# Reading 512-column products and scores from two places 1024 bytes apart, in a two-layer hybrid attention trunk on one Trainium2 core

## The chip, the cores and the metric

The kernel runs on one core of one Trainium2 chip. The time is the device time of one execution in microseconds, as the median of repeated runs. The profile is of one further execution. Its engines are called as in the trace: PE is TensorE's matrix multiply, PEld its weight load, DVE is VectorE, ACT is ScalarE, POOL is GpSimd and SP is SyncE, which issues the loads.

## The reference, cut to what matters

The program computes two layers over 256 tokens of width 1024 and a final RMS norm. Each layer normalises its input and multiplies it by one wide matrix. Out of that product come the queries, keys, values and gates of three causal attention mixers with 8 heads of 64 each, an index query and key, a weight per index head, a forget logit, and three merge gates.

```python
def hybrid_layer(x, gain, w_in, f_bias, w_branch, w_out):
    h = rms_norm(x, gain)
    proj = jnp.einsum('bsd,de->bse', h, w_in)
    # ... split into q, k, v, gate of a, b, c; q_idx, k_idx, w_idx; f_logit; merge_logit
    oa = moba_attention(...) * jax.nn.silu(ga)
    ob = dsa_attention(..., qi, ki, wi) * jax.nn.silu(gb)
    oc = forgetting_attention(...) * jax.nn.silu(gc)
    y = jnp.einsum('nbsw,nwd->bsnd', jnp.stack([oa, ob, oc], axis=0), w_branch)
    gates = jax.nn.sigmoid(merge_logit).reshape(B, S, N_BRANCH, D_MODEL)
    merged = jnp.sum(gates * y, axis=2)
    return x + jnp.einsum('bsd,de->bse', merged, w_out)
```

At 256 tokens mixer a is plain causal attention, mixer b keeps the 64 keys per query with the highest index score, which is a weighted sum over 8 index heads of relu(q_idx . k_idx), and mixer c adds a forgetting bias.

## The kernel before, in words

Everything is held to near float32 precision with products in a faster float format. A float32 operand is split into a high part, which ScalarE writes, and a low part, which VectorE gets by subtraction (`piece`, L345 to L368, for weights; `split_to`, L390, for activations). Each product is then three: high by high, low by high, high by low. So each weight piece of 128 x 1024 costs one instruction at L362 and one at L366, and three matmuls for each block of 128 rows.

Two functions make nearly all products. `unit_b` (L419) has the weights as the stationary operand and streams the 256 token columns of the normalised input; it makes queries, keys, gates and merge gates. `unit_a` (L435) has 128 tokens as the stationary operand and streams 512 weight columns; it makes the values of the mixers (`v_units`, L908) and the output projection (`w_out`), where the last 512 columns of the last token block are made as two units of 256. Both go through `mm_ops` (L401), so their matmuls all carry line L407. The values of the very first mixer are made by `first_v` (L922, matmuls at L954), which interleaves both token blocks as the weights arrive. `unit_y` (L833) makes the branch products.

The order in which a matmul reads its moving operand is a matter of the view. `turns` (in `hybrid_trunk`) turns a row of columns into pairs: column 0 of the first half, column 0 of the second half, column 1 of the first half, and so on. In `unit_b` and `unit_y` all 256-column products read this way already, from two places 512 bytes apart; their result lies pairwise in PSUM, and the readers undo it with `tiles`, which reads every second column (`plain` is the matching view of the destination). Products of 512 columns read their columns in order.

`scores` (L564) makes the scores of two heads against keys in one matmul: the key tile `bd` holds the two heads' keys 1024 bytes apart in each partition. For the first 128 queries it streams 2 x 128 columns, for the last 128 queries 2 x 256, three products each (L573 to L575). The result has head 0 in the first half and head 1 in the second. `attend` (L626) reads a head's scores with a VectorE instruction that adds the mask and takes the row extreme (L636), ScalarE takes the exponential (L640), the probabilities are transposed on TensorE (L663), split and multiplied by the values (L678 to L681). `index_scores` (L769) uses the same scores for the index heads: ScalarE writes the relu to an SBUF tile (L776, L777), VectorE sums the heads (L785, L787), and `select` (L790) takes the 64 highest by eight rounds of two instructions (L807, L808).

`v_out` (L915) writes the values' high and low parts to the tile `V` (L919, L920). The residual is added at L1039.

The order of the work is fixed ahead by a planner (`Plan.run`, L138). Each operation has a key, an engine and a price, and the planner simulates the engines and at each step writes out, on the engine that can start first, the ready operation of lowest key. A matmul's price is `t_mm` (L230), in ns for n columns. Buffers are taken and released in the same simulation, so a price moves the order on every engine.

At the end stands `forms` (L1047): 24 products of old data that nobody reads, in several read orders, planned behind everything else. The three buffers that they write are in turn s, s and t for every four products: 256 columns from four places and from eight places in turn, 256 columns from two places 1024 bytes apart, then 512 columns from two places 1024 bytes apart, from four places, and from two places 512 bytes apart within each half.

Of the kernel before, what the change touches and what calls it, by code (L numbers as in the profile page):

```python
# [227 lines left out]


def t_mm(n):  # L230
    return 1.3 + 0.4434 * n


@with_exitstack
def hybrid_trunk(ctx, tc, x, norm_gain, w_in, forget_bias, w_branch, w_out, final_gain, consts, out):
# [199 lines left out]
    def unit_a(name, gets, t, ah, al, ra, c=0, n=512):  # L435
        u = unit(name)
        ps = Buf("proj")
        o = lambda: T(ps)[:, :n]
        for i in range(4):
            p = gets[i](u)  # L440
            g = []
            for k in (2 * i, 2 * i + 1):
                wh = lambda p=p, k=k: p[0].v[:, k % 2, c:c + n]
                g += [(lambda k=k: ah(k, t), wh, [p[0]] + ra[0](k)), (lambda k=k: al(k, t), wh, [p[0]] + ra[1](k))]
            for k in (2 * i, 2 * i + 1):
                wl = lambda p=p, k=k: p[1].v[:, k % 2, c:c + n]
                g += [(lambda k=k: ah(k, t), wl, [p[1]] + ra[0](k))]
            mm_ops(o, g, t_mm(n), [ps], u, name, i == 0, i == 3, True)
        return u, ps
# [114 lines left out]
    def scores(q, k, ktoks, key):  # L564
        s0, s1 = Buf("s"), Buf("s")
        kt = [t for h in ktoks for t in h]

        def go():
            qh, ql = T(q[0]), T(q[1])
            kh, kl = T(k)  # L570
            for o, sl, n in ((T(s0)[:, :256], slice(0, 128), 128), (T(s1), slice(128, 256), 256)):
                o = o.rearrange("p (h c) -> p h c", h=2)
                PE.matmul(o, qh[:, sl], kh[:, :, :n], start=True, stop=False)  # L573
                PE.matmul(o, ql[:, sl], kh[:, :, :n], start=False, stop=False)  # L574
                PE.matmul(o, qh[:, sl], kl[:, :, :n], start=False, stop=True)  # L575
        pe(go, 3 * (t_mm(256) + t_mm(512)), [q[0], q[1], k] + kt, [s0, s1], key, "qk", MARGIN)
        return s0, s1

    class Pair:
# [46 lines left out]
        def attend(self, key):  # L626
            bs = [self.bias(h, key) for h in range(2)]
            s0, s1 = scores(self.q, self.k, self.kt, key)
            es, ke = [], []
            for h in range(2):  # L630
                b, bt, bb = bs[h]
                e, st = Buf("e"), Buf("st")
                kt = [Tok(), Tok()]
                parts = ((0, 0, 128, s0), (1, 128, 256, s1))
                for t, a, n, s in parts:
                    dve(lambda t=t, a=a, n=n, s=s, e=e, st=st, b=b, h=h: DVE.tensor_tensor_reduce(  # L636
                        T(e)[:, a:a + n], T(s)[:, h * n:(h + 1) * n], b()[:, a:a + n], 1.0, 3e38, ALU.add, ALU.min,
                        T(st)[:, t:t + 1]), n, [s, bt[t]], [kt[t]], key, "max", touch=[e, st] + bb)
                for t, a, n, s in parts:
                    act(lambda t=t, a=a, n=n, e=e, st=st: ACT.activation(  # L640
                        T(e)[:, a:a + n], T(e)[:, a:a + n], AF.Exp, bias=T(st)[:, t:t + 1], scale=-1.0,
                        accum_out=T(st)[:, 2 + t:3 + t]), n, False, [], [kt[t]], key, "exp", 185.0, touch=[e, st])
                for t, a, n, s in parts:
                    dve(lambda t=t, st=st: DVE.reciprocal(T(st)[:, 4 + t:5 + t], T(st)[:, 2 + t:3 + t]), 1, [], [kt[t]],
                        key, "recip", 75.0, touch=[st])

                    def on_act(t=t, a=a, n=n, e=e, st=st):
                        ACT.activation(T(e)[:, a:a + n], T(e)[:, a:a + n], AF.Copy, scale=T(st)[:, 4 + t:5 + t])

                    def on_dve(t=t, a=a, n=n, e=e, st=st):  # L650
                        DVE.tensor_scalar(T(e)[:, a:a + n], T(e)[:, a:a + n], T(st)[:, 4 + t:5 + t], None, op0=ALU.mult)  # L651
                    plan.op([("DVE", 129.0 + 0.52 * n, on_dve), ("ACT", t_act(n, False) + 93.0, on_act)], [], [kt[t]],
                            key, 0.0, "normalise", touch=[e, st]).port = True
                es.append(e)
                ke.append(kt)
            ph, pl = Buf("pth"), Buf("ptl")
            kp = [[Tok(), Tok()] for _ in range(2)]
            for h in range(2):
                ps = Buf("t")

                def tr(h=h, ps=ps):
                    for i in range(3):
                        PE.transpose(T(ps)[:, i * 128:(i + 1) * 128], T(es[h])[:, i * 128:(i + 1) * 128], ident)  # L663
                pe(tr, 330.0, ke[h] + [k_id], [ps], key, "pT", MARGIN, touch=[es[h]])
                src = lambda ps=ps: T(ps)[:, :384]
                act(lambda h=h, src=src: ACT.activation(T(ph)[:, h], src(), AF.Copy), 384, True, [ps],  # L666
                    [kp[h][0]], key, "pT", touch=[ph])
                dve(lambda h=h, src=src: DVE.tensor_tensor(T(pl)[:, h], src(), T(ph)[:, h].bitcast(F32), op=ALU.subtract),  # L668
                    384, [ps, kp[h][0]], [kp[h][1]], key, "pT", touch=[ph, pl])
            o = Buf("o")  # L670
            v = V[self.vi]

            def av():
                for h in range(2):
                    hd = 2 * self.p + h
                    ov = T(o)[:, h * S:(h + 1) * S]
                    a, b = slice(0, 256), slice(256, 384)
                    PE.matmul(ov, v[:, 0, hd], T(ph)[:, h, a], start=True, stop=False, skip_group_check=True)  # L678
                    PE.matmul(ov[:, 128:], v[:, 1, hd], T(ph)[:, h, b], start=False, stop=True, skip_group_check=True)
                    PE.matmul(ov[:64, 128:], v[:, 1, hd, :64], T(pl)[:, h, b], start=False, stop=False, skip_group_check=True)  # L680
                    PE.matmul(ov[:64], v[:, 0, hd, :64], T(pl)[:, h, a], start=False, stop=True, skip_group_check=True)  # L681
            kv = [t for p in k_V[self.vi] for t in p]
            pe(av, 700.0, kv + [ph, pl] + [t for h in kp for t in h], [o], key, "av", MARGIN)
            self.o, self.o_key = o, key
            if hasattr(self, "g"):
                self.gated()
# [82 lines left out]
    def index_scores(p, ps, kb, ktoks, key):  # L769
# [8 lines left out]
        for h in range(2):  # L778
            hd = 2 * p + h
            for t, (a, n) in enumerate(((0, 128), (128, 256))):  # L780
                rr = rel[t][:, h * n:(h + 1) * n]
                w = widx[:, t, hd:hd + 1]
                o = isc[:, a:a + n]
                if hd == 0:
# [128 lines left out]
            v_out(ps, t, vi, [ps], u)  # L913

    def v_out(ps, t, vi, deps, key):  # L915
        hi, lo = V[vi][:, t, :, :64], V[vi][:, t, :, 64:]
        src = lambda: T(ps).rearrange("p (h c) -> p h c", h=8)
        kv = [k for i in (2 * t, 2 * t + 1) for k in k_V[vi][i]]
        act(lambda: ACT.activation(hi, src(), AF.Copy), W, True, deps, kv, key, "v", touch=[ps])  # L919
        dve(lambda: DVE.tensor_tensor(lo, src(), hi.bitcast(F32), op=ALU.subtract), W, deps, kv, key, "v", touch=[ps])  # L920
# [1 line left out]
    def first_v():  # L922
# [5 lines left out]
        for i in range(4):  # L928
# [19 lines left out]
            for t in range(2):  # L948
                for w, h, kw, kx in ((ph, hA[0], kh, 0), (ph, hA[1], kh, 1), (pl, hA[0], kl, 0)):
                    for j in ((0,), (1,)) if i == 0 else ((0, 1),):  # L950
                        def emit(t=t, w=w, h=h, j=j, i=i, v3=v3):
                            for x in j:
                                left[t][0] -= 1
                                PE.matmul(T(ps[t]), h(2 * i + x, t), v3(w)[:, x], start=left[t][0] == 23, stop=left[t][0] == 0)  # L954
                        k = Tok()
                        done[t].append(k)
                        pe(emit, len(j) * t_mm(512), [kw[x] for x in j] + [k_hT[kx][t][2 * i + x] for x in j], [k], us[t] - 10,
# [41 lines left out]
    for l in range(L):  # L999
# [30 lines left out]
        for hh in range(2):  # L1030
            gets = [lambda k, i=i: rows_a("O", w_out, l, hh * 512, i, k) for i in range(4)]
            for t in range(2):
                ra = [lambda k, p=p: [k_mg[k][p]] for p in range(2)]
                cols = [(0, 256), (256, 256)] if last and hh + t == 2 else [(0, 512)]
                for i, (c, n) in enumerate(cols):
                    u, ps = unit_a(f"o{hh}{t}", gets, t, mA[0], mA[1], ra, c, n)
                    c += hh * 512
                    o = xs[t][:, c:c + n]
                    dve(lambda o=o, ps=ps, n=n: DVE.tensor_tensor(o, o, T(ps)[:, :n], op=ALU.add), n, [ps], [k_x[t][hh]],  # L1039
                        u - 4, "res")  # L1040
                    if last:
                        final_part(t, c, n, hh + i, u - 4, i == 1)
# [4 lines left out]
    def forms():  # L1047
# [4 lines left out]
        def emit():  # L1052
            bs = [T(x) for x in b]
            n = 0

            def go(m, w, v, k):
                nonlocal n
                for i in range(k):
                    x = v(f[:, i * w:(i + 1) * w])
                    y = x.shape  # L1060
                    o = bs[n % 3][:, :m]
                    o = o.rearrange("p (b a) -> p b a", a=y[2]) if len(y) == 3 else o.rearrange("p (c b a) -> p c b a", b=y[2], a=y[3])
                    PE.matmul(o, hTh[:, i, :128], x, start=True, stop=True)
                n += 1
            go(256, 256, lambda x: x.rearrange("p (a b) -> p b a", a=4), 4)
            go(256, 256, lambda x: x.rearrange("p (a b) -> p b a", a=8), 4)
            go(256, 512, lambda x: x.rearrange("p (a b) -> p b a", a=2)[:, :128], 4)
            go(512, 512, lambda x: x.rearrange("p (a b) -> p b a", a=2), 4)
            go(512, 512, lambda x: x.rearrange("p (a b) -> p b a", a=4), 4)
            go(512, 512, lambda x: x.rearrange("p (c a b) -> p c b a", c=2, a=2), 4)  # L1070
        pe(emit, 5000.0, [k_main] + hT_all[0] + hT_all[1], b, 10 ** 6, "forms")
    forms()
    PLAN_T.append(plan)
    PLAN_T[0] = plan.run({"PE": 0.0, "ACT": 0.0, "DVE": 0.0})
# [25 lines left out]
```

## Time and profile before

| | |
|---|---|
| median of 3 runs | 629.85 us (629.82 to 631.39) |
| profiled execution | 630.21 us |
| its span, first to last instruction | 628.4 us |
| TensorE busy | 615.5 us, 98% |
| VectorE busy | 543.7 us, 87% |
| ScalarE busy | 400.0 us, 64% |
| GpSimd busy | 85.4 us, 14% |
| granted TensorE clock | 1.0 |
| read from memory | 103.69 MB |

The span is what the views of the trace are measured in; the profiled execution's own time is 1.8 us longer, which lies outside the program's instructions. The chain of work that ended last is followed back from the last instruction, each time to what released it. Matmuls are pipelined: the length printed for one covers time in which the next already runs, so a product's price is read from the distance of starts.

### The profile page before, as it was taken

How to read it: one execution, taken by the hardware profiler on the slowest of the kernel's cores; microseconds unless marked ns; L12 is line 12 of the kernel's file. 1: busy time of each engine (PE TensorE's matmuls, PEld its weight loads, DVE VectorE, ACT ScalarE, POOL GpSimd, SP SyncE). 2: the span in 40 equal slices, each digit the busy share in tenths (PEclk: the TensorE clock that was granted, in tenths of full speed). 3: DMA queues.
4: the chain of work that ended last, by engine and by line, in shares of the span. 5: the costliest groups of instructions: out<-in, count | busy, mean ns of one | idle time of the engine just before them, and what ended most of it. 6: DMA issues, size and time to landing. Idle time of an engine off the chain costs nothing.

```text
span 628.4 us, 12640 instructions
## 1 busy us (share of the span) xinstructions
PE 615.5 (98%) x4860; PEld 584.3 (93%) x4860; DVE 543.7 (87%) x1334; ACT 400.0 (64%) x797; POOL 85.4 (14%) x98
## 2 busy tenths in 40 slices
PE   7999989999999999999999998999999999999999
PEld 6999989899998999899889998998999999999988
DVE  8899998986978989899588999989698898989873
ACT  5775576666756667575487656767567674847641
POOL 1342120100000221200004303020000012211001
PEclk9999999999999999999999999999999999999999
DMA  8845638455472562665545545565736455363701
GB/s 295 275 144 163 202 100 270 136 168 172 149 251 68 177 193 68 201 216 187 155 150 184 170 136 166 158 212 167 227 109 202 137 161 160 107 210 101 267 34 68
DMA packets 93853, 105.56 MB, mean 168 GB/s; under 512 B 4320, under 2 KB 82400, under 8 KB 93792
## 3 DMA queue, kind: packets, MB, share of 16 engines
q1 hardware_dynamic: 93504, 104.36, 52.1%
q8 instruction: 38, 0.62, 0.4%
q10 hardware_dynamic: 288, 0.39, 0.2%
q14 instruction: 23, 0.19, 0.1%
HBM read 103.69 MB, written 1.05 MB: 167 GB/s over the span
## 4 chain that ended last, share of the span: by engine, by line
PE 71%; DVE 21%; ACT 4%; DMA 2%; issue 1%; SPq 0%; ACTq 0%; DVEq 0%
PE proj L407 61%; DVE wl L366 8%; PE t L663 2%; ACT e L640 2%; DVE isc L808 2%; PE proj L954 2%; DVE t L807 1%; DMA raw<-in_w_out_dram 1%; PE s L573 1%; PE s L575 1%; PE s L574 1%; DVE rsh L455 1%; DVE rr L457 1%; DVE isc L787 1%; DVE e L636 1%
## 5 line engine op out<-in xcount | busy, mean ns | idle before, releaser
L366 DVE TENSOR_TENSOR wl<-raw,wh 128x1024 fp32r<-128x1024 f32 (+1 forms) x190 | 234.7, 1247 | 30.9 <-ACT wh L362 29.7
L407 PE MATMUL proj<-hTh,wh 128*128 128x256 f32 (+1 forms) x1040 | 247.0, 277 | 2.1 <-DVE g L602 1.7
L407 PE MATMUL proj<-hTl,wh 128*128 128x256 f32 (+1 forms) x1040 | 245.7, 275 | 0.0
L362 ACT ACTIVATE wh<-raw 128x1024 fp32r<-128x1024 f32 (+1 forms) x190 | 197.8, 1055 | 71.2 <-PE proj L407 49.1
L407 PEld LDWEIGHTS proj<-hTh,wh 128*128 128x128 f32 (+1 forms) x1040 | 199.0, 191 | 3.9 <-DVE g L602 2.5
L407 PEld LDWEIGHTS proj<-hTl,wh 128*128 128x128 f32 (+1 forms) x1040 | 199.2, 192 | 0.7
L407 PE MATMUL proj<-hTh,wl 128*128 128x256 f32 (+1 forms) x1040 | 160.1, 277 | 0.0
L407 PEld LDWEIGHTS proj<-hTh,wl 128*128 128x128 f32 (+1 forms) x1040 | 137.9, 191 | 1.3
L456 POOL TENSOR_TENSOR rsh<-rsh,cst 128x256 f32<-128x256 f32 (+1 forms) x42 | 35.3, 840 | 380.0 <-DVE rsh L455 380.0
L640 ACT ACTIVATE e<-e,st 128x128 f32<-128x128 f32 x96 | 42.6, 445 | 19.3 <-DVE st L636 19.2
L458 POOL TENSOR_TENSOR rr<-rr,rsh 128x256 f32<-128x256 f32 (+1 forms) x42 | 43.4, 1032 | 15.6 <-ACT mth L824 6.0
L407 PE MATMUL proj<-wh,v 128*128 128x512 f32 (+1 forms) x144 | 35.6, 368 | 0.0
L407 PE MATMUL proj<-og0l,wh 128*128 128x256 f32 x128 | 32.2, 277 | 0.3 <-DVE og0l L398 0.3
L407 PE MATMUL proj<-wh,hTh 128*128 128x512 f32 x80 | 32.3, 404 | 0.0
L407 PE MATMUL proj<-og0h,wh 128*128 128x256 f32 x128 | 32.1, 277 | 0.0
L407 PE MATMUL proj<-wh,hTl 128*128 128x512 f32 x80 | 31.5, 394 | 0.0
L694 ACT ACTIVATE ot<-o 64x256 f32<-64x256 f32 x48 | 18.3, 381 | 19.5 <-PE o L681 19.0
L407 PEld LDWEIGHTS proj<-wh,v 128*128 128x128 f32 x144 | 25.2, 188 | 4.7
L663 PE MATMUL t<-cst,e 128*128 128x128 f32 x144 | 24.5, 279 | 1.8 <-DVE e L651 1.2
L668 DVE TENSOR_TENSOR ptl<-t,pth 128x384 fp32r<-128x384 f32 x48 | 25.2, 550 | 0.7 <-ACT pth L666 0.3
L407 PEld LDWEIGHTS proj<-og0l,wh 128*128 128x128 f32 x128 | 24.6, 192 | 0.7 <-DVE og0l L398 0.5
L407 PE MATMUL proj<-wl,hTh 128*128 128x512 f32 x80 | 24.9, 392 | 0.0
(195 smaller groups left out, 1023.8 us busy)
## 6 DMA issues: line engine op xcount, KB each, us to landing
raw<-in_w_in_dram SPq DMA_DIRECT2D x74, 1024.0 KB, 5.2
raw<-in_w_branch_dram SPq DMA_DIRECT2D x24, 512.0 KB, 4.9
raw<-in_w_out_dram SPq DMA_DIRECT2D x8, 1024.0 KB, 5.8
raw<-in_w_in_dram SPq DMA_DIRECT2D x3, 512.0 KB, 7.1
x<-in_x_dram SPq DMA_DIRECT2D x4, 256.0 KB, 4.5
raw<-in_w_in_dram SPq DMA_DIRECT2D x2, 320.0 KB, 5.8
out_dram<-tmp SPq DMA_DIRECT2D x2, 320.0 KB, 2.4
raw<-in_w_in_dram SPq DMA_DIRECT2D x2, 256.0 KB, 4.4
```

Of the source, the lines that this page charges most:

```text
L362: ACT.activation(p[0].v, sel(c.v), AF.Copy)
L366: DVE.tensor_tensor(p[1].v, sel(c.v), p[0].v.bitcast(F32), op=ALU.subtract)
L407: PE.matmul(o(), a(), b(), start=first and i == 0, stop=last and i == n - 1)
L455: dve(lambda: DVE.stream_shuffle(T(sh)[:np_], a(), SWAP), S, [ps], [sh], key, "rope")
L456: gps(lambda: POOL.tensor_tensor(T(sh)[:np_], T(sh)[:np_], s[:np_], op=ALU.mult), S, [k_rope], [sh], key, "rope")
L458: gps(lambda: POOL.tensor_tensor(T(r)[:np_], T(r)[:np_], T(sh)[:np_], op=ALU.add), S, [sh], [r], key, "rope")
L640: act(lambda t=t, a=a, n=n, e=e, st=st: ACT.activation(T(e)[:, a:a + n], T(e)[:, a:a + n], AF.Exp, bias=T(st)[:, t:t + 1], scale=-1.0, acc ...
L663: PE.transpose(T(ps)[:, i * 128:(i + 1) * 128], T(es[h])[:, i * 128:(i + 1) * 128], ident)
L668: dve(lambda h=h, src=src: DVE.tensor_tensor(T(pl)[:, h], src(), T(ph)[:, h].bitcast(F32), op=ALU.subtract), 384, [ps, kp[h][0]], [kp[h][1 ...
L694: act(lambda r=r, h=h: ACT.activation(T(t)[r], T(o)[64:, h * S:(h + 1) * S], AF.Copy), S, True, [o], [kt[h]], key, "og", HALF, touch=[t])
L808: dve(lambda o=o, t8=t8: DVE.match_replace(o, T(t8), o, TAKEN), n, [t8], [k_isc[i]], key + r * step, "top8")
L954: PE.matmul(T(ps[t]), h(2 * i + x, t), v3(w)[:, x], start=left[t][0] == 23, stop=left[t][0] == 0)
```

## The change: what it does

Products of 512 columns in `unit_a` and `first_v` read their columns through `turns`, so from two places 256 columns, that is 1024 bytes, apart in turn. The two `unit_a` units of 256 columns at the end read from two places 512 bytes apart. The result lies pairwise in PSUM: `v_out` and the residual add read it with a step of two columns. In `scores` the keys of the two heads are read in turn, and the result has the heads in turn; the score maximum at L636 and the index sum at L785 and L787 read every second column.

The planner's price of a product changes: for 256 columns from 114.8 to 111.6 ns, for 512 from 228.3 to 216.3 ns. The unread products at the end are others: 28 in place of 24.

```diff
 def t_mm(n):
-    return 1.3 + 0.4434 * n
+    return 7.0 + 0.4087 * n
...
     def unit_a(name, gets, t, ah, al, ra, c=0, n=512):
-        o = lambda: T(ps)[:, :n]
+        o = lambda: T(ps)[:, :n].rearrange("p (b a) -> p b a", a=2)
...
-                wh = lambda p=p, k=k: p[0].v[:, k % 2, c:c + n]
+                wh = lambda p=p, k=k: turns(p[0].v[:, k % 2, c:c + n])
...
-                wl = lambda p=p, k=k: p[1].v[:, k % 2, c:c + n]
+                wl = lambda p=p, k=k: turns(p[1].v[:, k % 2, c:c + n])
...
     def scores(q, k, ktoks, key):
-                o = o.rearrange("p (h c) -> p h c", h=2)
-                PE.matmul(o, qh[:, sl], kh[:, :, :n], start=True, stop=False)
-                PE.matmul(o, ql[:, sl], kh[:, :, :n], start=False, stop=False)
-                PE.matmul(o, qh[:, sl], kl[:, :, :n], start=False, stop=True)
+                o = o.rearrange("p (c h) -> p c h", h=2)
+                mh, ml = (x[:, :, :n].rearrange("p h c -> p c h") for x in (kh, kl))
+                PE.matmul(o, qh[:, sl], mh, start=True, stop=False)
+                PE.matmul(o, ql[:, sl], mh, start=False, stop=False)
+                PE.matmul(o, qh[:, sl], ml, start=False, stop=True)
...
     def attend(self, key):
-                        T(e)[:, a:a + n], T(s)[:, h * n:(h + 1) * n], b()[:, a:a + n], 1.0, 3e38, ALU.add, ALU.min,
+                        T(e)[:, a:a + n], T(s)[:, :2 * n].rearrange("p (c h) -> p h c", h=2)[:, h], b()[:, a:a + n], 1.0, 3e38, ALU.add, ALU.min,
...
     def index_scores(p, ps, kb, ktoks, key):
-                rr = rel[t][:, h * n:(h + 1) * n]
+                rr = rel[t].rearrange("p (c h) -> p h c", h=2)[:, h]
...
     def v_out(ps, t, vi, deps, key):
-        hi, lo = V[vi][:, t, :, :64], V[vi][:, t, :, 64:]
-        src = lambda: T(ps).rearrange("p (h c) -> p h c", h=8)
+        hi, lo = (V[vi][:, t, :, c:c + 64].rearrange("p (a h) c -> p a h c", a=2) for c in (0, 64))
+        src = lambda: T(ps).rearrange("p (h c a) -> p a h c", h=4, a=2)
...
     def first_v():
-                                PE.matmul(T(ps[t]), h(2 * i + x, t), v3(w)[:, x], start=left[t][0] == 23, stop=left[t][0] == 0)
+                                PE.matmul(T(ps[t]).rearrange("p (b a) -> p b a", a=2), h(2 * i + x, t), turns(v3(w)[:, x]), start=left[t][0] == 23, stop=left[t][0] == 0)
...
-                    dve(lambda o=o, ps=ps, n=n: DVE.tensor_tensor(o, o, T(ps)[:, :n], op=ALU.add), n, [ps], [k_x[t][hh]],
+                    dve(lambda o=o, ps=ps, n=n: DVE.tensor_tensor(plain(o), plain(o), tiles(T(ps)[:, :n]), op=ALU.add), n, [ps], [k_x[t][hh]],
...
     def forms():
-            go(256, 256, lambda x: x.rearrange("p (a b) -> p b a", a=4), 4)
-            go(256, 256, lambda x: x.rearrange("p (a b) -> p b a", a=8), 4)
-            go(256, 512, lambda x: x.rearrange("p (a b) -> p b a", a=2)[:, :128], 4)
-            go(512, 512, lambda x: x.rearrange("p (a b) -> p b a", a=2), 4)
-            go(512, 512, lambda x: x.rearrange("p (a b) -> p b a", a=4), 4)
-            go(512, 512, lambda x: x.rearrange("p (c a b) -> p c b a", c=2, a=2), 4)
-        pe(emit, 5000.0, [k_main] + hT_all[0] + hT_all[1], b, 10 ** 6, "forms")
+            go(256, lambda i: f[:, i * 256:i * 256 + 256].rearrange("p (c a b) -> p c b a", c=2, a=2), 4)
+            go(256, lambda i: f[:, i * 64:i * 64 + 768].rearrange("p (a b) -> p b a", a=2)[:, :128], 4)
+            go(256, lambda i: f[:, i * 64:i * 64 + 1024].rearrange("p (a b) -> p b a", a=2)[:, :128], 4)
+            go(256, lambda i: f[:, i * 256:i * 256 + 264].rearrange("p (a b) -> p b a", a=2)[:, :128], 4)
+            go(256, lambda i: f[:, i * 256:i * 256 + 288].rearrange("p (a b) -> p b a", a=2)[:, :128], 4)
+            go(512, lambda i: f[:, i * 64:i * 64 + 1024].rearrange("p (a b) -> p b a", a=2)[:, :256], 4)
+            go(128, lambda i: f[:, i * 256:i * 256 + 128].rearrange("p (a b) -> p b a", a=2), 4)
+        pe(emit, 4000.0, [k_main] + hT_all[0] + hT_all[1], b, 10 ** 6, "forms")
```

More of the change, by code (lines that the diff above doesn't have):

```diff
@@ L1054, in emit, with go @@
             n = 0
-            def go(m, w, v, k):
+            def go(m, v, k):
                 nonlocal n
                 for i in range(k):
-                    x = v(f[:, i * w:(i + 1) * w])
+                    x = v(i)
                     y = x.shape
                     o = bs[n % 3][:, :m]
-                    o = o.rearrange("p (b a) -> p b a", a=y[2]) if len(y) == 3 else o.rearrange("p (c b a) -> p c b a", b=y[2], a=y[3])
+                    if len(y) == 3:
+                        o = o.rearrange("p (b a) -> p b a", a=y[2])
+                    elif len(y) == 4:
+                        o = o.rearrange("p (c b a) -> p c b a", b=y[2], a=y[3])
                     PE.matmul(o, hTh[:, i, :128], x, start=True, stop=True)
                 n += 1
-            go(256, 256, lambda x: x.rearrange("p (a b) -> p b a", a=4), 4)
-            go(256, 256, lambda x: x.rearrange("p (a b) -> p b a", a=8), 4)
-            go(256, 512, lambda x: x.rearrange("p (a b) -> p b a", a=2)[:, :128], 4)
-            go(512, 512, lambda x: x.rearrange("p (a b) -> p b a", a=2), 4)
-            go(512, 512, lambda x: x.rearrange("p (a b) -> p b a", a=4), 4)
-            go(512, 512, lambda x: x.rearrange("p (c a b) -> p c b a", c=2, a=2), 4)
-        pe(emit, 5000.0, [k_main] + hT_all[0] + hT_all[1], b, 10 ** 6, "forms")
+            go(256, lambda i: f[:, i * 256:i * 256 + 256].rearrange("p (c a b) -> p c b a", c=2, a=2), 4)
[6 more added lines that the diff above has]
+        pe(emit, 4000.0, [k_main] + hT_all[0] + hT_all[1], b, 10 ** 6, "forms")
     forms()
```

## The prediction

> **What bounds the kernel now.** I read the page's busy line and its chain of work first, then the busy time by stretches cut where the chain changes engine, then the matmuls in order of time.
>
> ```profile
> span 628.4 us, 12640 instructions
> PE 615.5 (98%) x4860; PEld 584.3 (93%) x4860; DVE 543.7 (87%) x1334; ACT 400.0 (64%) x797; POOL 85.4 (14%) x98
> PE 71%; DVE 21%; ACT 4%; DMA 2%; issue 1%; SPq 0%; ACTq 0%; DVEq 0%
> ```
>
> TensorE is busy nearly all the time and carries 71% of the chain; VectorE carries 21%. The next view, busy time in stretches, shows where (columns: stretch, length, then PE, PEld, DVE, ACT, POOL busy with instruction counts, granted clock, DMA share, GB/s):
>
> ```profile
> 47.70:87.50 39.80, 37.16 (x315) 36.01 (x315) 39.59 (x120) 22.17 (x41) 9.81 (x12) 1.00 0.53 165
> 87.50:223.70 136.20, 136.18 (x1109) 130.71 (x1108) 117.25 (x273) 89.80 (x186) 9.92 (x11) 1.00 0.55 174
> 223.70:253.20 29.50, 28.53 (x248) 27.66 (x246) 27.21 (x73) 21.06 (x46) 6.04 (x8) 1.00 0.35 103
> 284.60:359.90 75.30, 75.25 (x504) 68.20 (x505) 61.21 (x129) 48.69 (x83) 12.91 (x15) 1.00 0.51 161
> 359.90:391.80 31.90, 30.32 (x261) 29.49 (x260) 31.77 (x108) 17.03 (x31) 5.83 (x9) 1.00 0.52 163
> 391.80:530.70 138.90, 138.88 (x1134) 133.50 (x1133) 118.84 (x276) 90.73 (x188) 11.53 (x13) 1.00 0.54 171
> ```
>
> In the long stretches (136, 75 and 139 us) TensorE never rests and VectorE has 14 to 20 us to spare: a shorter matmul there ends the stretch sooner. In the selection stretches (40 and 32 us) VectorE is full (39.59 of 39.80) and TensorE waits some 2 us in each: a shorter matmul there only waits longer. The clock is 1.00 everywhere, so matmul time is set by the instruction, not by throttling.
>
> **What a product costs now, and in the new order.** A busy matmul's printed length overlaps the next one, so I use distances between starts. The tail of the timeline holds all the forms needed. First the last output products in order of time (columns: start, length, engine, line, names, shape, count), then a look at 625.0 us that separates two of the unread products at L1063:
>
> ```profile
> 606.74 1.08 PE L407 MATMUL proj<-wh,v 128*128 128x512 f32 x4
> ...
> 616.40 0.63 PE L407 MATMUL proj<-wh,v 128*128 128x256 f32 x4
> ...
> 622.06 1.61 PE L1063 MATMUL s<-hTl,hTh 128*128 128x256 f32 x8
> 623.49 0.63 PE L1063 MATMUL t<-hTl,hTh 128*128 128x256 f32 x4
> 623.96 2.15 PE L1063 MATMUL s<-hTl,hTh 128*128 128x512 f32 x8
> 625.94 1.03 PE L1063 MATMUL t<-hTl,hTh 128*128 128x512 f32 x4
> ```
>
> ```profile
> 624.83 0.43 PE L1063 MATMUL s<-hTl,hTh 128*128 128x512 f32 x1
> ```
>
> From 606.74 to 616.40 the program issues 42 products of 512 contiguous columns: 9.66 us / 42 = 230 ns each. From 616.40 to 622.06 there are 48 of 256 contiguous columns: 5.66 / 48 = 118 ns. The unread products at L1063 already contain the new order: the first four of 512 columns read two places 256 elements, that is 1024 bytes, apart in turn, and take 623.96 to 624.83, 217 ns each. The next four, which go through four places, take 624.83 to 625.94, 278 ns. So not every order is good, but the one chosen is 13 to 14 ns below the contiguous one. (The eight products of 256 columns at 622.06, four and eight places in turn, average 179 ns.) That the gain survives beside the other engines' traffic is seen from the 256-column products, which already alternate between places 512 bytes apart: one piece of the chain of waits (start, length, what),
>
> ```profile
> 174.85 9.39 PE proj L407 x84
> ```
>
> is 9.39 / 84 = 112 ns each in the middle of the kernel, against 118 contiguous.
>
> The counts, from the instruction groups by shape (count | busy us, mean ns | idle before):
>
> ```profile
> L407 PE MATMUL proj<-wh,hTh 128*128 128x512 f32 x80 | 32.3, 404 | 0.0
> L407 PE MATMUL proj<-wh,v 128*128 128x512 f32 x112 | 30.5, 394 | 0.0
> L407 PE MATMUL proj<-wh,v 128*128 128x256 f32 x32 | 5.1, 280 | 0.0
> L954 PE MATMUL proj<-wh,hTh 128*128 128x512 f32 x16 | 5.4, 407 | 2.3 <-DVE small L478 1.6 <-ACT hTh L515 0.7
> L574 PE MATMUL s<-bd0h,ql 128*128 128x512 f32 x12 | 4.7, 395 | 0.0
> ```
>
> Each product is made of three terms (high by high, low by high, high by low), so values through unit_a are 3 x 80 = 240 products; the output is 112 + 56 = 168 of 512 columns and 32 + 16 = 48 of 256; first_v has 3 x 16 = 48. Scores are made 32 times (24 head pairs, 8 index pairs; the L574 row holds those of one of three key buffers), each with three products of 256 and three of 512 columns: 96 of each. The order inside one group of scores:
>
> ```profile
> 117.49 0.28 PE L575 MATMUL s<-bd1l,qh 128*128 128x256 f32 x1
> 117.61 0.39 PE L573 MATMUL s<-bd1h,qh 128*128 128x512 f32 x1
> 117.83 0.40 PE L574 MATMUL s<-bd1h,ql 128*128 128x512 f32 x1
> ```
>
> 120 ns for 256, 220 for 512 with the two-digit rounding of this view: the contiguous prices above within 10 ns. Their two heads also lie 1024 bytes apart; the third unread form (623.49, 256 columns from places 1024 bytes apart) takes 0.47 / 4 = 117 with its first product and I take 112, the price of the alternated 256 above.
>
> **The change part by part.**
>
> Values and output in unit_a: 408 products x 13.5 ns = 5.5 us, nearly all in stretches where TensorE sets the end. The 48 of 256 columns at the very end: 48 x 6 = 0.3 us, on the path.
>
> first_v: 48 x 13.5 = 0.65 us; its first half waits for weights and activations (the idle 2.3 us in its row), so 0.4.
>
> Scores: 96 x 13.5 + 96 x 6 = 1.9 us. Index scores and many attention scores lie in stretches that VectorE sets; I take half, 0.9, between ends of 0.3 and 1.9.
>
> Readers of the reordered results: v_out, the residual add and the score maximum now read every second PSUM column, the index sum L787 every second SBUF element. What such a read costs, from groups that already do it (the first of each pair reads with a step, the second does not):
>
> ```profile
> L398 DVE SCALAR_TENSOR_TENSOR ql<-proj,qh 128x256 fp32r<-128x256 f32 x8 | 3.4, 421 | 0.0
> L850 DVE SCALAR_TENSOR_TENSOR acc<-acc,proj 128x256 f32<-128x256 f32 x16 | 6.6, 414 | 0.4
> L397 ACT ACTIVATE qh<-proj 128x256 fp32r<-128x256 f32 x8 | 3.0, 374 | 2.0 <-PE proj L407 1.9
> L821 ACT ACTIVATE acc<-proj 128x256 f32<-128x256 f32 x16 | 6.1, 379 | 11.2 <-PE proj L407 11.2
> L397 ACT ACTIVATE v<-acc 128x256 fp32r<-128x256 f32 x16 | 7.2, 474 | 10.1 <-DVE acc L857 10.1
> L397 ACT ACTIVATE og0h<-ot 128x256 fp32r<-128x256 f32 x16 | 6.7, 417 | 7.7 <-DVE ot L699 6.7 <-POOL ot L698 0.8
> ```
>
> and the index sum as it is now:
>
> ```profile
> L787 DVE SCALAR_TENSOR_TENSOR isc<-tmp,widx,isc 128x256 f32<-128x256 f32 x14 | 7.7, 551 | 0.0
> ```
>
> From PSUM the step costs nothing on either engine (421 to 414, 374 to 379 ns), so the first three groups are put at 0; at 7 ns each the 96 maxima would cost 0.7 us. From SBUF it costs ScalarE 57 ns per 256. Index sums: 32, between 0 and 57 ns each, 0 to 1.8 us, inside the stretches VectorE sets; I take 0.8. The Trainium skill (SBUF — State Buffer, Door 1) says SBUF delivers 16-byte lines and that two hits in a line suffice; a step of 8 bytes would then be free, and this term 0. The ScalarE pair disagrees with it.
>
> The planner's matmul price falls from 114.8 to 111.6 ns for 256 columns and from 228.3 to 216.3 for 512. It writes out every engine's order, so some orders will shift. No row prices this; the nearest are TensorE's longest single waits for VectorE (engine, waiting line, cause: total us, times, longest):
>
> ```profile
> PE s L575 <- DVE bd1l L712: 2.0, 1, 2.0
> PE s L575 <- DVE bd2l L712: 1.3, 1, 1.3
> ```
>
> One such wait gained or lost: -2 to +2 us; I take 0, as the new price is nearer to the measured distances and points neither way.
>
> The unread products at the end: 24 become 28 (20 of 256, 4 of 512, 4 of 128 columns). They run behind the last output product, beside the final norm and the output transfer:
>
> ```profile
> L560 ACTq DMA_DIRECT2D out_dram<-tmp x2: 350/362/375, 620.0 to 624.8; - x2
> DMA to landing us min/median/max: 2.0/2.4/2.6
> ```
>
> The transfer issued at 624.8 lands by 627.4, while the last unread product ends at 625.94 + 1.03 = 627.0. The cover is 627.4 - 622.06 = 5.3 us. The new set takes 20 x 112 + 4 x 217 + 4 x 112 = 3.6 us, or with 179, 278 and 179 ns 5.4 us: 0 to 0.1 us; I take 0. It does move the last busy instruction, so the page's chain may end on another engine.
>
> Sum: 5.5 + 0.3 + 0.4 + 0.9 - 0.8 = 6.3 us off. The profiled execution took 630.2 us (span 628.4 and 1.8 around it), so 623.9; the median of the runs is 0.4 below that execution, so 623.5.
>
> **The rivals.**
>
> (1) VectorE takes over more. With TensorE faster, its 87% becomes 88%, and the stretches where both are over 90% grow; or a shifted order adds a wait like the two above. For it: PE stands still only some 2 us in each selection stretch, so the engines are close there. Against: the long stretches have 14 to 20 us of VectorE slack. Scores then bring nothing, a wait of 2 us comes in: 6.3 - 0.9 - 2 = 3.4 off, 626.5; 2 to 5 off in all.
>
> (2) Nothing arrives, within 0.3%: the alternated order costs the same once the weights are being written next to it. The 256-column rows speak against it. 629.9.
>
> (3) Slower: the score maximum (L636, 96 instructions) reads PSUM with a step in an operation that no row shows with one. At half speed (135 ns per 128 columns, from the rows below) a head costs 405 ns more, 48 heads 19.4 us of VectorE; with two fifths of it where VectorE sets the end (my choice between none and all), 8 us: 631.5. It decides from 6.3 / (0.4 x 48) = 330 ns per head on.
>
> ```profile
> L636 DVE CUSTOM_DVE_ANT_0 e<-s,cst 128x256 f32<-128x256 f32 x16 | 6.7, 417 | 0.0
> L636 DVE CUSTOM_DVE_ANT_0 e<-s,cst 128x128 f32<-128x128 f32 x16 | 4.5, 282 | 0.0
> ```
>
> (4) Slower by much: reading from two places loses time in each product, as four places do. At 278 instead of 230 ns, 552 products cost 26 us more: 656. The same section of the Trainium skill speaks for this: each access that leaves its line pays a penalty, and here every access does. By that rule the change loses; the four products at 623.96 and the 112 ns products show it does not hold for two places.
>
> **How the numbers follow.** The forecast (5 to 8.5 us off) gets 0.64, rival 1 0.24, rival 2 0.06, rival 3 0.04, rival 4 0.02. A measurement of this kernel tells 0.3%, 1.9 us, from no change. Faster is the forecast and rival 1: 0.88; same 0.07, with a little of rival 3; slower 0.05. Time 623.5. Upper end: rival 1 with the index sums at their 1.8 us, 627.2. Lower end: all of first_v and the scores, index sums free (8.3 us off), and half a wait gained, 620.6.
>
> **What would show it.** Distances of 217 ns between starts of 512-column products at L407 and L954, and of 112 in the last 48, would confirm the main term; 230 means rival 2, 278 rival 4. L636 at 417 and 282 ns refutes rival 3. L787 (551 ns for 256 now) shows the index term. TensorE's list of waits and the selection stretches (39.8 and 31.9 us now) show whether VectorE took the gain: if products cost 217 and the time falls by less than 5 us, the planner's order or VectorE is where it went. The forecast fails if the products get their price but long new waits on L712 or L366 appear.

## The result and the profile after

The changed kernel takes 619.37 us (618.74 to 620.75, 4 runs) against 629.84 us before (629.40 to 631.39, 4 runs): a ratio of 0.9832, 95% interval 0.9807 to 0.9858, or 10.5 us less. The forecast was 623.5 with a range of 620.6 to 627.2: the sign was right, the gain 1.7 times the predicted one, and the time lies under the range.

The page of the kernel after (span, busy time, chain by engine):

```profile
span 618.6 us, 12635 instructions
PE 606.7 (98%) x4864; PEld 584.7 (95%) x4864; DVE 540.0 (87%) x1319; ACT 407.0 (66%) x814; POOL 82.2 (13%) x96
PE 70%; DVE 20%; ACT 1%; issue 1%; ACTq 0%; DVEq 0%
```

The shares look as before, but one thing the edits of the reads did not touch has moved: VectorE has 15 instructions fewer, ScalarE 17 more, GpSimd 2 fewer. With the new prices the planner put work on other engines: the normalisation of the probabilities has a form for VectorE and one for ScalarE, and those on ScalarE (L649, L648 before) rise from 23 to 40; two gate products moved from GpSimd to VectorE.

The products have the price that the prediction read from the unread ones. The last output products in order of time, kernel after (start, length, engine, line, names, shape, count):

```profile
600.40 1.03 PE L407 MATMUL proj<-wh,v 128*128 128x512 f32 x4
...
606.87 0.61 PE L407 MATMUL proj<-wh,v 128*128 128x256 f32 x4
...
612.23 0.50 PE L1067 MATMUL s<-hTl,hTh 128*128 128x256 f32 x3
```

30 products of 512 columns from 600.40 to 606.87 are 216 ns each (230 before), 48 of 256 from 606.87 to 612.23 are 112 (118 before). The readers, by shape (count | busy us, mean ns | idle before), kernel after:

```profile
L637 DVE CUSTOM_DVE_ANT_0 e<-s,cst 128x256 f32<-128x256 f32 x16 | 6.7, 420 | 0.0
L637 DVE CUSTOM_DVE_ANT_0 e<-s,cst 128x128 f32<-128x128 f32 x16 | 4.5, 284 | 0.0
L788 DVE SCALAR_TENSOR_TENSOR isc<-tmp,widx,isc 128x256 f32<-128x256 f32 x14 | 7.0, 497 | 0.0
L788 DVE SCALAR_TENSOR_TENSOR isc<-tmp,widx,isc 128x128 f32<-128x128 f32 x14 | 5.8, 415 | 0.0
```

The score maximum reads every second PSUM column at 420 and 284 ns (417 and 282 before). The index sum, put at up to 57 ns more, got shorter: 497 ns from 551. The experiments show that the new order did this, and that the step by itself made it longer.

TensorE's waits of before at the scores, 2.0 and 1.3 us for L712, are gone from its list; of what is left there, the longest and the one at the scores are these (engine, waiting line, cause: total us, times, longest):

```profile
PE proj L407 <- DVE wl L366: 2.3, 3, 1.4
PE proj L955 <- DVE wh L945: 1.7, 1, 1.7
...
PE s L576 <- DVE bd0l L713: 0.5, 1, 0.5
```

So the products explain part, and an order with fewer waits may explain the rest. The experiments take the two apart. Each run is compared with runs of the kernel before on the same chip, which lay between 630.0 and 630.4 us in the median. In some executions the granted clock falls to half for 3.4 us, as the traces below show; their mean clock then reads 0.997 or less, and most of them take longer.

### The profile page after: what moved, and what is told of

It reads as the page before. It is cut to its first block, busy times and chain, and to the rows that moved or that the text cites. A ratio compares the mean times of both kernels' runs of the same rounds, so it can differ in the third digit from the quotient of the medians.

```text
span 618.6 us, 12635 instructions
## 1 busy us (share of the span) xinstructions
PE 606.7 (98%) x4864; PEld 584.7 (95%) x4864; DVE 540.0 (87%) x1319; ACT 407.0 (66%) x814; POOL 82.2 (13%) x96
## 4 chain that ended last, share of the span: by engine, by line
PE 70%; DVE 20%; ACT 1%; issue 1%; ACTq 0%; DVEq 0%
PE proj L407 60%; DVE wl L366 7%; PE t L664 2%; DVE isc L809 2%; DVE t L808 1%; PE s L574 1%; PE s L576 1%; PE s L575 1%; DVE e L637 1%; DVE mth L856 1%; DVE acc L858 1%; DVE v L398 1%; PE o L679 1%; PE o L682 1%; ACT wh L362 1%
## 5 line engine op out<-in xcount | busy, mean ns | idle before, releaser
L456 POOL TENSOR_TENSOR rsh<-rsh,cst 128x256 f32<-128x256 f32 (+1 forms) x42 | 33.5, 796 | 403.5 <-DVE rsh L455 401.9
L407 PE MATMUL proj<-og0h,wl 128*128 128x256 f32 x128 | 24.8, 275 | 0.0
L407 PEld LDWEIGHTS proj<-og0h,wh 128*128 128x128 f32 x128 | 24.6, 192 | 0.0
```

The source lines that it names most:

```text
L407: PE.matmul(o(), a(), b(), start=first and i == 0, stop=last and i == n - 1)
L456: gps(lambda: POOL.tensor_tensor(T(sh)[:np_], T(sh)[:np_], s[:np_], op=ALU.mult), S, [k_rope], [sh], key, "rope")
```

## Experiments: reads and order taken apart

The planner's price and the read order are independent edits, and the order of the instructions, with the engine of those that have a choice, follows from the prices alone. So four kernels separate them.

**All reads changed, old prices** (instruction for instruction the order of before):

```diff
 def t_mm(n):
-    return 7.0 + 0.4087 * n
+    return 1.3 + 0.4434 * n
```

> All read orders of the change, with the planner's matmul price of before (1.3 + 0.4434 n), so that every engine gets the order of before, instruction for instruction. Theory A (two parts that add up: the products' price, about 8.3 us, and a better order, 2 to 2.7 us): 621.5 us, 8 us below before, with the waits at the scores (L574 to L576) and transposes (L664) as long as before, about 5 and 4 us. Theory B (the shorter products alone shorten the waits, the order does nothing): 619 us, as the changed kernel, with the waits down to 2 and 1 us. Theory C (the prediction's: some of the products' price is lost in stretches that VectorE sets): 622.5 to 623.5.

Measured: 625.99 us, ratio 0.9929 (0.9912 to 0.9946), 4.0 us off. All three theories missed; even theory C, the prediction's, had 6.5 to 7.5 us off. The median mixes two kinds: three executions at full clock took 624.97 to 625.08 us, three at 0.995 took 626.90 to 627.25. At full clock the kernel before took 629.27 to 630.26 on this chip, so the gain there is 4.5 us between medians, still short of theory C.

**New prices, old reads** (the kernel before with the line above the other way round, so the order of the changed kernel):

> The kernel before with nothing but the planner's new matmul price, so the order of the changed kernel with all products read as before. Theory A: 627 us, 2 to 2.7 us below before, products of 512 columns still 230 ns apart. Theory B: 629.6, no difference from before.

Measured: 625.94 us, ratio 0.9935 (0.992 to 0.995), 4.1 us off. An edit that changes no product, only two numbers in the planner, is worth as much as all the faster products in the old order. The two numbers change the order and, with it, the engine of 19 small operations: this kernel has the same counts of instructions on VectorE, ScalarE and GpSimd as the change (1319, 814 and 96). How much comes from the order and how much from these moves was not taken apart. Theory B falls. Theory A was right that the order counts, but had it too small, and wrong that the two parts add up: 4.0 and 4.1 alone, 10.5 together.

**Products without scores** (the changed kernel with L570 to L576, the score maximum and the index sum as before):

```diff
-                o = o.rearrange("p (c h) -> p c h", h=2)
+                o = o.rearrange("p (h c) -> p h c", h=2)
...
-                rr = rel[t].rearrange("p (c h) -> p h c", h=2)[:, h]
+                rr = rel[t][:, h * n:(h + 1) * n]
```

> The changed kernel with the scores, the score maximum and the index sum as before; values and output products read alternated; the order of the changed kernel. If the price of the scores arrives in full: 620.9, 1.9 us above the changed kernel. If half of it is hidden where VectorE sets the end, as the prediction has it: 619.9. If all of it is hidden: 619.0.

Measured: 619.25 us, ratio 0.9825 (0.9811 to 0.984), the same as the whole change.

**Scores alone** (the kernel before with the new prices and the changed scores):

> The kernel before with the new planner's price and with the scores alone read alternated (with score maximum and index sum); values and output products contiguous. Theory A with the scores' price in full: 625.1, 1.9 us below the run that has the new prices alone; half: 626.1; none: 627. If reading with a step cost VectorE anything, it would be above 627 and L637 above 420 ns.

Measured: 626.02 us, ratio 0.9934 (0.9919 to 0.9949), the same as the new prices alone. Between the medians the scores' share is not seen from either side. At a mean clock of 0.999 or 1.00 it is about half a microsecond: 625.17 to 625.43 us here against 625.77 to 625.98 with the new prices alone, and, in separate measurements, 618.74 and 618.82 in the change against 618.97 to 619.53 with the products only. Three of the six executions here and two of the four of the change had a lower clock (0.997), and the medians hide the difference.

Where each microsecond went is read from the distances between starts of consecutive matmuls, summed by kind of product from the end of first_v to the last output product; a wait counts with the product before it. This table is worked out from the traces of one execution each:

```
us, by kind of product          before  reads,   prices,  products change
                                        old pr.  old rd.  only
512 columns, unit_a       x408   95.1    90.0     97.4     91.9    92.1
256 columns, last ones    x48     5.7     5.4      5.7      5.4     5.4
scores of 512             x96    22.1    21.2     22.7     22.6    21.3
scores of 256             x96    16.5    16.2     12.9     12.9    12.6
transposes of e           x144   16.8    17.3     13.2     13.3    13.5
256 columns, all others   x3696 419.7   422.0    419.7    419.8   420.3
all else                         23.4    23.6     23.6     23.6    23.6
sum                             599.3   595.7    595.2    589.5   588.8
```

Down the second column: the unit_a products get 5.1 us shorter and the scores 1.2, but 2.3 us come back at the 256-column products and 0.5 at the transposes. Not all of this is waiting. The execution behind this column had the clock at half from 81.21 to 84.62 us, behind the 2.4 us wait at the scores (columns: stretch, length, PE, PEld, DVE, ACT, POOL busy with counts, clock, DMA share, GB/s):

```profile
81.21:84.62 3.41, 3.41 (x16) 3.23 (x15) 3.38 (x16) 0.96 (x5) 1.48 (x2) 0.50 0.94 303
```

The 256-column products there start every 213 ns in place of 112, which makes some 1.3 of the 2.3 us; new waits for VectorE make about 1.2, and a wait of 0.3 us that the kernel before has is gone. What a column at full clock would show is not on record; the 4.5 us between executions at full clock say that the loss does not hang on the clock alone. Third column: the new prices alone take 3.6 us from the 256-column scores and 3.6 from the transposes. There the list of the kernel before has waits of 3.3 us for VectorE and of 1.8 us for VectorE and ScalarE; the new prices give 2.3 us back at the 512-column products. Third to fourth: 5.5 us and 0.3 us, the full price of the products, with nothing coming back. Fourth to fifth: the scores get 1.3 and 0.3 us shorter, and 0.9 us of it returns at the other rows.

The place where the old order spends the faster products shows in the busy time of one stretch, 204 to 285 us, with the clock at 1.00 (columns as above). Kernel before:

```profile
204.00:285.00 81.00, 79.21 (x685) 77.02 (x684) 74.03 (x176) 54.26 (x113) 14.57 (x16) 1.00 0.55 175
```

All reads changed, old prices:

```profile
204.00:285.00 81.00, 78.71 (x684) 76.82 (x682) 74.34 (x176) 54.92 (x113) 14.63 (x16) 1.00 0.54 175
```

New prices, old reads:

```profile
204.00:285.00 81.00, 81.00 (x709) 79.89 (x708) 73.24 (x175) 56.63 (x116) 14.07 (x16) 1.00 0.54 175
```

In the old order TensorE stands still 1.79 us of this stretch, and 2.29 once its products are shorter: there it waits for VectorE, and the shorter products wait longer. In the new order TensorE is busy all 81.00 us and has 24 matmuls more in the same time; VectorE is busy 0.8 us less and ScalarE 2.4 us more. TensorE is the bound there, and what it saves is saved. The list of TensorE's waits with the reads changed and the old prices agrees:

```profile
PE proj L407 <- DVE g L603: 2.9, 4, 0.9
PE s L576 <- DVE bd1l L713: 2.4, 1, 2.4
```

1.7 became 2.9 us for the gate at L602 (L603 here), 2.0 became 2.4 at the scores. Two of the four waits for the gate are new, 0.6 us each at 220 and 523 us, one in each layer. The first lies in the long stretch in which the kernel before keeps TensorE busy 136.18 of 136.20 us; with the reads changed and the old prices it is

```profile
87.50:223.70 136.20, 135.48 (x1112) 131.24 (x1111) 117.79 (x273) 90.38 (x188) 10.30 (x10) 1.00 0.54 172
```

## Experiments: is the new order better for a reason?

**Prices 1% up, and 1% down** (products read as in the change):

```diff
-    return 7.0 + 0.4087 * n
+    return (7.0 + 0.4087 * n) * 1.01
```

> The changed kernel with the planner's matmul prices raised by 1% (112.7 and 218.5 ns); products read as in the change, another order. Theory A (the order got better because the price of a 256-column product now agrees with the measured 111.6 ns): within 1.5 us of 619.3, or a little above. Theory L (each order is a draw; the one of the change happened to be good): anywhere from 617 to 626.

> The changed kernel with the planner's matmul prices lowered by 1% (110.5 and 214.1 ns). Theory A: within 1.5 us of 619.3. Theory L: anywhere from 617 to 626.

**One price old, one new:**

```diff
-    return 7.0 + 0.4087 * n
+    return 114.8 if n == 256 else 7.0 + 0.4087 * n
```

> The changed kernel with the planner's old price for 256 columns (114.8 ns, measured 111.6) and the new one for 512 (216.3, measured 216). Theory A: as with both old prices, 625 to 626, since some 3,700 of the products have 256 columns and the scores and transposes wait for VectorE again. If the price of the 512-column products is what counts: 619 to 620. Theory L: no relation.

and the same with `228.3 if n == 512`:

> The changed kernel with the planner's new price for 256 columns and the old one for 512 (228.3 ns, measured 216). Theory A: close to the changed kernel, 619 to 621. If the 512 price counts: 625 to 626. Theory L: no relation.

**The kernel before with prices 1% up, and 1% down:**

> The kernel before with its planner's matmul prices raised by 1% (115.9 and 230.6 ns); products read as before. Theory A (distance from the measured 111.6 ns of a 256-column product costs time): 630 to 632. Theory L (an order is a draw with a spread of some us): anywhere from 625 to 633.

> The kernel before with its planner's matmul prices lowered by 1% (113.7 and 226.0 ns). Theory A: 628 to 630. Theory L: anywhere from 625 to 633.

Measured, sorted by the price of a 256-column product (it takes 111.6 ns on the chip):

| price of 256 / 512 columns, ns | reads | time, us | ratio to before (95%) |
|---|---|---|---|
| 110.5 / 214.1 | changed | 624.48 | 0.9905 (0.9891 to 0.992) |
| 111.6 / 216.3 (the change) | changed | 619.37 | 0.9832 (0.9807 to 0.9858) |
| 111.6 / 228.3 | changed | 621.24 | 0.9854 (0.984 to 0.9869) |
| 112.7 / 218.4 | changed | 620.97 | 0.9848 (0.9833 to 0.9863) |
| 114.8 / 216.3 | changed | 625.55 | 0.9917 (0.9882 to 0.9952) |
| 114.8 / 228.3 | changed | 625.99 | 0.9929 (0.9912 to 0.9946) |
| 111.6 / 216.3 | old | 625.94 | 0.9935 (0.992 to 0.995) |
| 113.7 / 226.0 | old | 629.99 | 0.9996 (0.9982 to 1.0009) |
| 114.8 / 228.3 (before) | old | 629.84 | 1 |
| 116.0 / 230.6 | old | 638.51 | 1.0134 (1.0111 to 1.0156) |

With the same products, the prices alone, through the order and the engine of some small operations, move the time by 6.6 us with the changed reads and by 12.6 us with the old. There is a trend that theory A would have: every order with 256 columns at 114.8 ns or more is at least 3.9 us worse than the best of its group, and the price of the 512-column products counts less. But 1% below the measured price costs 5.1 us, where theory A expected under 1.5, and 1% above the old one ended at 638.51, outside what either theory expected (630 to 632 and 625 to 633). The row of 625.55 is a mixture of clocks: at 0.999 and 1.00 that kernel took 623.36 and 623.41 us, less than the 624.34 to 624.94 of the price 1% low. So the distance from the measured price explains a part; the rest looks like a draw, as theory L has it. What decides a single draw was not found. The number of instructions on ScalarE does not: it is 814 in the best order, 811 in the one of 624.48 and 808 in that of 620.97, and of the old reads the order with 808 (629.99 us) is no faster than the one with 797 (629.84).

**The worst draw** is 8.3 us above the kernel before on the same chip. TensorE's waits in the kernel before with prices 1% up:

```profile
PE proj L407 <- ACT og0h L397: 3.9, 2, 1.9
PE s L575 <- DVE bd2l L712: 1.9, 2, 1.5
```

and the stretches at and behind three of them (columns as above, the granted clock is the number behind POOL):

```profile
284.60:286.60 2.00, 0.20 (x2) 0.00 (x1) 1.60 (x3) 0.70 (x2) 0.00 (x0) 1.00 0.72 271
287.00:291.50 4.50, 4.42 (x25) 4.31 (x25) 2.81 (x8) 1.79 (x3) 0.00 (x0) 0.62 0.65 235
387.60:389.30 1.70, 0.29 (x2) 0.08 (x1) 1.67 (x5) 0.00 (x0) 0.81 (x1) 1.00 0.65 217
390.00:393.50 3.50, 3.50 (x17) 3.36 (x17) 3.50 (x18) 1.50 (x7) 0.78 (x2) 0.53 0.13 30
595.90:597.90 2.00, 0.21 (x2) 0.02 (x1) 1.61 (x3) 0.70 (x2) 0.00 (x0) 1.00 0.76 286
598.50:601.80 3.30, 3.30 (x15) 3.30 (x16) 1.27 (x3) 0.55 (x2) 0.00 (x0) 0.50 0.88 313
```

Behind waits of 1.5 to 1.9 us the clock is granted at half for some 3.4 us, though TensorE is busy by then: 15 products of 256 columns in 3.3 us, 220 ns each where 112 is usual. An estimate from these: such a wait costs TensorE its own length and some 1.6 us more. This is not the whole of the 8.3 us. The execution shown has three such stretches and took 640.39 us; the one of the four that took least, at a mean clock of 0.997, still took 637.88.

## Experiments: the clock at the start, and the step

The profiled execution of the changed kernel has such a stretch at its start, with the clock at 0.53 (row below), the profiled one of before has not. It may be one reason why the changed kernel's runs spread over 2 us: the two executions with a mean clock of 0.997 took 619.92 and 620.75 us, the other two 618.74 and 618.82.

```profile
12.60:15.90 3.30, 3.30 (x11) 2.66 (x11) 2.85 (x3) 2.01 (x4) 0.33 (x1) 0.53 1.11 333
```

**Work in the wait at the start:** 7 unread products, 14 matmuls in the trace, are put behind the first products of `first_v`.

```diff
+                        if i == 0 and t == 0 and kx == 1 and j == (1,):
+                            def busy():
+                                for _ in range(7):
+                                    PE.matmul(T(idle)[:, :128], ones, ones, start=True, stop=True)
+                            idle = Buf("o")
+                            pe(busy, 10.0, [k], [idle], us[0] - 11, "busy")
```

> The changed kernel with 7 more unread products of 128 columns put behind the first six products of first_v, where TensorE waits 1.7 us at 9.2 us; the order of all other work is the same. Theory K (the drop of the granted clock to 0.5 from 12.8 to 16.2 us in the profiled execution of the changed kernel follows from that wait and costs 1.7 us in some executions): the clock is 1.0 in every execution, 618.7 us, and the spread of the runs shrinks from 2 us to under 1. Rival (the drop has nothing to do with the wait): median 619.4 with clocks of 0.997 in some runs as before.

Measured: 619.30 us (618.59 to 619.74), ratio 0.9825 (0.9807 to 0.9844). The clock was 1.00 in all five executions, and the same stretch of the trace has it at 1.00:

```profile
12.60:15.90 3.30, 3.30 (x21) 2.90 (x20) 3.10 (x5) 3.25 (x9) 0.02 (x1) 1.00 1.12 335
```

21 matmuls instead of 11 in 3.3 us. The spread fell to 1.2 us, where theory K expected under 1, and the median is the same as without, where it expected 618.7: what theory K says of the clock is seen, its gain in time is not. The changed kernel's own clocks were 1.000, 0.999 and twice 0.997 over its four executions, so five at 1.00 are a sign and no proof.

**The step moved to ScalarE:** the relu of the index scores undoes the pairs.

```diff
-        act(lambda: ACT.activation(rel[1], T(s1), AF.Relu), 512, ...
+        act(lambda: ACT.activation(plain(rel[1]), tiles(T(s1)), AF.Relu), 512, ...
...
-                rr = rel[t].rearrange("p (c h) -> p h c", h=2)[:, h]
+                rr = rel[t][:, h * n:(h + 1) * n]
```

> The changed kernel with the relu of the index scores undoing the pairs (ScalarE reads PSUM with a step), so that the index sum L788 reads contiguous SBUF again; same order. If reading SBUF with a step costs VectorE what the prediction took (25 ns of 0 to 57 each): L788 25 ns shorter than in the changed kernel (497 and 415 ns) and up to 0.8 us off. If the step is free and the length of L788 follows from what else runs: lengths within 10 ns of those, time the same.

Measured: 619.27 us, ratio 0.9826 (0.9806 to 0.9846), no difference. The index sums by shape, contiguous again:

```profile
L788 DVE SCALAR_TENSOR_TENSOR isc<-tmp,widx,isc 128x256 f32<-128x256 f32 x14 | 6.6, 472 | 0.0
L788 DVE SCALAR_TENSOR_TENSOR isc<-tmp,widx,isc 128x128 f32<-128x128 f32 x14 | 5.7, 408 | 0.0
```

25 ns and 7 ns shorter than with the step, 0.4 us in all: the size that the prediction took for 256 columns, less for 128, and not seen in the time. The other pairs agree: with the old prices the step makes the 256-column sum 571 ns from 551, and with the new ones 497 from 475.

## Why the prediction was right or wrong, point by point

- **Price of the products: right.** 230 to 217 ns read, 231 to 216 measured (medians); the last 48 from 118 to 112. Theirs was 5.8 us; in the new order 5.5 + 0.3 us arrived. Rivals 2 and 4 fall, and with rival 4 the line rule of the Trainium skill (SBUF — State Buffer, Door 1) as a rule for this operand: every read of the alternated order leaves its line and the products got faster, not slower.
- **first_v: too low, by a little.** 0.4 taken; 0.75 measured between two executions at full clock, with new prices and the reads old and changed (its end at 22.2 and 21.5 us).
- **Scores: too high, inside the bounds.** 0.9 taken between 0.3 and 1.9; no difference between the medians with and without them, about 0.5 us between executions at full clock, 0.7 us between the traces of the last two columns of the table. Their products did get their price (230 to 216 ns, 1.6 us), and 0.9 us of it came back in other rows. The reason given, stretches that VectorE sets, fits this and was not tested by itself.
- **Index sum: right in kind, too high.** 0.8 us of cost taken, 25 ns for each sum; the step costs 20 to 25 ns for 256 columns and 5 to 9 for 128, 0.4 us in all, and none of it is seen in the time. The group became 1.9 us shorter all the same, since the new order with the old reads takes the 256-column sum from 551 to 475 ns, for a reason that was not looked for.
- **Rival 3: refuted.** 420 and 284 ns against 417 and 282.
- **The unread products at the end: right.** 0 taken; from the first of them to the end of the span are 6.3 us before (622.06 to 628.4) and 6.4 after (612.23 to 618.6), so their other number and forms are no part of the gain.
- **The planner's price: the step that failed.** It was bounded at -2 to +2 us by one of TensorE's longest waits and taken as 0. Alone it takes off 4.1 us, outside its bounds. The bound was mis-built: a new price does not move one wait but writes all of them anew, and with them the choice of engine for 19 operations. Six orders of the changed reads spread over 6.6 us, four of the old reads over 12.6. The text had seen that the new price is nearer to the measured distance, and set it aside.
- **Adding the terms: wrong too.** The gross 7.1 us of the reads were expected whatever the order; in the old order 4.0 arrive, in the new 6.6 (625.94 to 619.37). A part of the missing 3 us is the half clock behind a wait (at full clock 4.5 arrive). Another part is new waits where the prediction saw none: the stretches with 14 to 20 us of VectorE slack were read as safe, but slack over a stretch of 136 us says nothing of a chain within 30 of them. In the old order the shorter products meet a new wait of 0.6 us for VectorE inside the first of these stretches, and one inside the last. What else keeps the products' price back in the old order was not taken apart.
- **The upper end of the range is mis-added.** Rival 1 with its 3.4 us off, less the 1.0 us more that the index sums cost at 1.8, is 2.4 us off: 627.5 and not 627.2. The measured time lies at the other end, so nothing rests on it.

## What to carry to other kernels

A number in a planner is an edit to every engine's order: price it by running the old order with the new operations and the new order with the old ones, before crediting the operations. A faster product is worth its price only where TensorE waits for nobody; look for idle time in the stretch, not for slack on the other engine. And when 1% on a price moves the time by 5 us, compare a handful of neighbouring prices before keeping one.

## What the runs showed of the hardware that was not expected

- **Order of the moving operand.** 512 columns read contiguously start every 231 ns, in turn from two places 1024 bytes apart every 216 ns; 256 columns 118 and 112 ns. The Trainium skill (TensorE: Matmul & The Clock Gate, Part 1) gives N / 2.4 GHz + 2.5 ns, 215.7 ns, for 512 columns back to back: the alternated products here meet it, the contiguous ones miss it by 15 ns. The new unread products at the end of the changed kernel show the same for 256 columns from places 256, 528, 576, 1536 and 2048 bytes apart. Their pieces in its chain (start, length, what):

```profile
612.39 0.89 PE s L1067 x8
613.29 0.45 PE t L1067 x4
613.74 0.89 PE s L1067 x8
```

Twenty products in 2.23 us are 112 ns each, and the distances between starts are 111 to 112 ns in all five forms; 512 columns from places 2048 bytes apart take 216 ns. Four places in turn took 278 ns for 512 columns in the kernel before.
- **Half clock behind short waits.** Waits of 1.5 to 2.4 us were followed by 3.4 us at half the granted clock in several executions, in one case two waits of 0.8 and 0.9 us close together (the old price for 256 columns, at 89.9 us). Not all such waits were: the 2.0 us wait of the kernel before at L575 was not, in the profiled execution. The Trainium skill (TensorE: Matmul & The Clock Gate, Part 1) has the drop after an idle window of about 3.4 us; here TensorE was idle for 1.6 to 2.4 us of the 3.4 before each drop.
